# Sixty-six empty drains at the head of VectorE's program in a rotary embedding on one core

## Chip, cores, metric

One core of one Trainium2 chip. The metric is the device time of one execution in microseconds (us), the median over runs. A comparison of two kernels is a ratio with a 95% interval; it is the mean time of the one kernel's fast runs over that of the other's of the same rounds, so not quite the ratio of the medians quoted beside it.

## The reference

```python
# x: (8, 2048, 8, 64) float32; cos, sin: (2048, 32) float32
def reference(x, cos, sin):
    x1, x2 = x[..., :32], x[..., 32:]
    cos, sin = cos[None, :, None, :], sin[None, :, None, :]
    return np.concatenate([x1 * cos - x2 * sin, x1 * sin + x2 * cos], axis=-1)
```

34 MB are read and 34 MB written; there are four multiplications for each pair of values.

## The kernel before

Each of 8 batches is one tile of 128 partitions by 8192 values. Five such tiles are loaded ahead; each later load reuses a tile once its store has landed. The tables are loaded behind the first piece of batch 0. VectorE copies the cosines to PSUM first, because all its multiplies read them there:

```python
    def load(b):
        xt = xpool.tile([P, ROW], f32, tag="xt", name=f"xt{b}")
        for lo, n in spans([UNIT, UNIT, 2 * UNIT] if b == 0 else [ROW]):
            keep(nc.sync.dma_start(out=xt[:, lo : lo + n], in_=xv[b, :, lo : lo + n]))
            if b == 0 and lo == 0:
                keep(nc.sync.dma_start(out=cos_sb, in_=cos_src))
                keep(nc.sync.dma_start(out=sin_sb, in_=sin_src))
    # ... (cut)
    for b in range(NBUF):            # NBUF = 5
        load(b)
    # ... (cut: GpSimd makes an identity)
    keep(nc.scalar.mul(nsin, sin_sb, -1.0))
    keep(nc.scalar.copy(sin_ps, sin_sb))
    keep(nc.scalar.mul(neye, eye, -1.0))
    keep(nc.vector.tensor_copy(cos_ps, cos_sb))
```

For most pieces GpSimd makes x·sin into `t2`, VectorE makes x·cos into `t1` and adds the two in place. For a few pieces TensorE adds, and ScalarE copies the sum back. A batch is stored whole, except for the first and the last, which are stored in parts:

```python
    for b in range(B):
        done = 0
        outs = list(spans(shares(b)))
        for lo, n in spans(pieces(b)):
            rotate(b, lo, n)
            done = lo + n
            while outs and sum(outs[0]) <= done:
                store(b, *outs.pop(0))
        if b + NBUF <= last:
            load(b + NBUF)
```

`keep` holds an instruction at its place in the program's order. A scheduling layer adds the waits and gives out the semaphores.

Of the kernel before, what the change touches and what calls it, by code (L numbers as in the profile page):

```python
# [10 lines left out]
def kernel(  # L11
# [7 lines left out]
    nc = tc.nc  # L19
    keep = tc.keep_in_program_order  # L20
# [68 lines left out]
    keep(nc.scalar.mul(nsin, sin_sb, -1.0))  # L89
    keep(nc.scalar.copy(sin_ps, sin_sb))  # L90
    keep(nc.scalar.mul(neye, eye, -1.0))
    keep(nc.vector.tensor_copy(cos_ps, cos_sb))  # L92

    def rep(a, n):
# [125 lines left out]
```

## Time and profile before

| | before |
|---|---|
| median of the first three runs | 163.42 us (163.28 to 164.14) |
| span of the profiled run | 161.4 us |
| VectorE, GpSimd busy | 140.1 us (87%), 139.0 us (86%) |
| DMA | 67.65 MB, mean 419 GB/s |
| VectorE's copy of the cosines starts | 6.20 us |
| the last store is issued, has landed | 153.3 us, 160.6 us |

### The profile page before, as it was taken

What the parts mean: (1) busy time and instruction counts of PE and PEld (TensorE: products, weight loads), DVE (VectorE), ACT (ScalarE), POOL (GpSimd) and SP (SyncE); (2) the same over time, 40 slices, a digit from 0 to 9 for tenths busy, and PEclk for the clock granted to TensorE, in tenths of its full rate; (3) what the DMA queues carried; (4) which work ended last, traced back from release to release, by engine and by line L of the source; (5) the groups of instructions that cost most, each with busy time, mean ns of one, the idle gap of its engine ahead of it and who ended that gap; (6) DMA issues with size and microseconds to landing.
All of it is one profiled execution on the core that took longest, in us unless ns stands there. A gap on an engine that the chain in (4) does not pass through costs nothing.

```text
span 161.4 us, 467 instructions
## 1 busy us (share of the span) xinstructions
PE 46.4 (29%) x80; PEld 18.5 (11%) x80; DVE 140.1 (87%) x66; ACT 14.4 (9%) x24; POOL 139.0 (86%) x70
## 2 busy tenths in 40 slices
PE   0000000498008960893029912980000000000000
PEld 0000000133003420340014401430000000000000
DVE  0468899999999999999999999999899998999900
ACT  3200000013000220032001210140000000000000
POOL 1299999999999899998996999998999979999200
PEclk9999999999955696599755985799555555555555
DMA  5999999899999999999999999999999999999995
GB/s 181 418 445 464 449 430 390 373 427 499 406 390 447 430 487 390 447 438 414 447 422 430 447 416 438 447 406 447 455 392 455 447 398 455 438 406 455 410 398 231
DMA packets 3458, 67.65 MB, mean 419 GB/s; under 512 B 384, under 2 KB 384, under 8 KB 768
## 3 DMA queue, kind: packets, MB, share of 16 engines
q1 hardware_dynamic: 1728, 34.08, 49.8%
q10 hardware_dynamic: 1728, 33.56, 48.4%
q14 instruction: 2, 0.02, 0.0%
HBM read 34.08 MB, written 33.55 MB: 419 GB/s over the span
## 4 chain that ended last, share of the span: by engine, by line
DMA 46%; DVE 37%; POOL 9%; issue 2%; SPq 1%; DVEq 0%; POOLq 0%; ACTq 0%
DMA xt<-in_x_dram 24%; DVE t L128 18%; DMA out_dram<-xt 18%; DVE xt L135 17%; POOL t L121 9%; DMA sin_sb<-in_sin_dram 3%; DVE t L145 1%; SPq L69 0%; SPq L67 0%; DVEq L135 0%; POOLq L121 0%; ACTq L74 0%
## 5 line engine op out<-in xcount | busy, mean ns | idle before, releaser
L121 POOL TENSOR_TENSOR t<-xt,sin_sb 128x1024 f32<-128x1024 f32 (+1 forms) x32 | 70.4, 2200 | 10.7 <-DMA sin_sb<-in_sin_dram 5.7
L128 DVE TENSOR_TENSOR t<-xt,cos_ps 128x2048 f32<-128x2048 f32 (+1 forms) x34 | 73.4, 2166 | 0.8
L121 POOL TENSOR_TENSOR t<-xt,nsin 128x1024 f32<-128x1024 f32 (+1 forms) x32 | 70.4, 2200 | 0.0
L135 DVE TENSOR_TENSOR xt<-t,t 128x2048 f32<-128x2048 f32 (+1 forms) x29 | 62.2, 2144 | 6.2 <-POOL t L121 3.7
L140 PE MATMUL o<-t,eye 128*128 128x512 f32 x24 | 17.1, 803 | 25.2 <-DVE t L128 25.2
L156 PE MATMUL o<-t,eye 128*128 128x512 f32 x16 | 10.9, 781 | 36.8 <-DVE t L128 36.8
L141 PE MATMUL o<-t,eye 128*128 128x512 f32 x24 | 15.0, 710 | 0.0
L142 ACT COPY xt<-o 128x512 f32<-128x512 f32 x12 | 7.0, 586 | 46.5 <-PE o L141 46.5
L140 PEld LDWEIGHTS o<-t,eye 128*128 128x128 f32 x24 | 5.6, 247 | 33.5 <-issue 33.5
L161 ACT COPY xt<-o 128x512 f32<-128x512 f32 x8 | 4.7, 586 | 42.6 <-PE o L157 42.6
L156 PEld LDWEIGHTS o<-t,eye 128*128 128x128 f32 x16 | 3.6, 247 | 41.7 <-POOL t L121 30.6
L141 PEld LDWEIGHTS o<-t,eye 128*128 128x128 f32 x24 | 5.9, 248 | 8.5 <-issue 8.5
L92 DVE COPY cos_ps<-cos_sb 128x512 f32<-128x512 f32 x1 | 0.7, 695 | 6.2 <-DMA cos_sb<-in_cos_dram 6.2
L157 PE MATMUL o<-t,neye 128*128 128x512 f32 x8 | 4.9, 714 | 0.2 <-DVE t L145 0.2
L145 DVE TENSOR_TENSOR t<-xt,sin_ps 128x2048 f32<-128x2048 f32 x2 | 4.6, 2279 | 0.0
L157 PE MATMUL o<-t,eye 128*128 128x512 f32 x8 | 4.1, 592 | 0.0
L157 PEld LDWEIGHTS o<-t,neye 128*128 128x128 f32 x8 | 1.8, 239 | 3.6 <-issue 3.6
L157 PEld LDWEIGHTS o<-t,eye 128*128 128x128 f32 x8 | 1.5, 190 | 1.9 <-issue 1.9
L89 ACT ACT_TABLE_LOAD x1 | 1.3, 1283 | 0.7 <-PEq L204 0.7
L89 ACT ACTIVATE nsin<-sin_sb 128x512 f32<-128x512 f32 x1 | 0.6, 629 | 4.9 <-DMA sin_sb<-in_sin_dram 4.9
L90 ACT COPY sin_ps<-sin_sb 128x512 f32<-128x512 f32 x1 | 0.6, 580 | 0.0
L79 POOL MEMSET eye<- 128x128 f32 x1 | 0.2, 205 | 0.3 <-POOLq L204 0.3
(6 smaller groups left out, 1.0 us busy)
## 6 DMA issues: line engine op xcount, KB each, us to landing
xt<-in_x_dram SPq DMA_DIRECT2D x7, 4096.0 KB, 38.9
out_dram<-xt ACTq DMA_DIRECT2D x6, 4096.0 KB, 28.3
out_dram<-xt ACTq DMA_DIRECT2D x2, 2048.0 KB, 18.9
xt<-in_x_dram SPq DMA_DIRECT2D x2, 1024.0 KB, 6.0
xt<-in_x_dram SPq DMA_DIRECT2D x1, 2048.0 KB, 11.5
out_dram<-xt ACTq DMA_DIRECT2D x2, 1024.0 KB, 8.7
out_dram<-xt ACTq DMA_DIRECT2D x1, 1792.0 KB, 20.4
cos_sb<-in_cos_dram SPq DMA_DIRECT2D x1, 256.0 KB, 5.0
```

The lines of the kernel that those rows point to most:

```text
L89: keep(nc.scalar.mul(nsin, sin_sb, -1.0))
L92: keep(nc.vector.tensor_copy(cos_ps, cos_sb))
L121: nc.gpsimd.tensor_mul(out=t2u[:, :, u, :].rearrange("p (r h) d -> p r h d", h=H), in0=xu[:, :, 1 - u, :].rearrange("p (r h) d -> p r h d" ...
L128: nc.vector.tensor_mul(out=t1.rearrange("p (r k d) -> p r k d", r=nr, d=Dh), in0=xk, in1=rep(cos_ps[:, r0 : r0 + nr, :], 2 * H),)
L135: keep(nc.vector.tensor_add(out=xt, in0=t1, in1=t2))
L140: nc.tensor.matmul(o, eye, t1[:, cs], start=True, stop=False)
L141: nc.tensor.matmul(o, eye, t2[:, cs], start=False, stop=True)
L142: keep(nc.scalar.copy(xt[:, cs], o))
L145: nc.vector.tensor_mul(out=t2.rearrange("p (r k d) -> p r k d", r=nr, d=Dh), in0=xk, in1=rep(sin_ps[:, r0 : r0 + nr, :], 2 * H),)
L156: nc.tensor.matmul(o, eye, t1u[:, gs, u, :], start=True, stop=False)
L157: nc.tensor.matmul(o, eye if u else neye, t2u[:, gs, 1 - u, :], start=False, stop=True)
L161: nc.scalar.copy(xu[:, gs, u, :], o.rearrange("p (g d) -> p g d", d=Dh))
```

## The change

The intent is to learn whether instructions that do nothing, put where VectorE waits for a load anyway, are free. A drain (`nc.vector.drain()`) names no tile. The profile lists it under DVEq, with VectorE's semaphore instructions, and does not count it as busy time of VectorE, which is 140.1 us before.

```diff
     keep(nc.scalar.mul(neye, eye, -1.0))
+    for _ in range(66):
+        keep(nc.vector.drain())
     keep(nc.vector.tensor_copy(cos_ps, cos_sb))
```

## The prediction

> **What bounds the kernel now.** I read the page first for the shares of the engines and of the DMA, then the timeline of the first 22 us, because the change acts only at the head of VectorE's program, then VectorE's waits and GpSimd's, and last the chain of waits, for what an extra instruction of the sequencer costs.
>
> The page, with the busy shares (section 1), the DMA row by 40 slices of about 4 us, the traffic by queue, and the issues of the stores:
>
> ```profile
> PE 46.4 (29%) x80; PEld 18.5 (11%) x80; DVE 140.1 (87%) x66; ACT 14.4 (9%) x24; POOL 139.0 (86%) x70
> DMA  5999999899999999999999999999999999999995
> HBM read 34.08 MB, written 33.55 MB: 419 GB/s over the span
> q14 instruction: 2, 0.02, 0.0%
> out_dram<-xt ACTq DMA_DIRECT2D x2, 1024.0 KB, 8.7
> ```
>
> The reader is to see that the DMA is full from the second slice to the last but one. The bytes alone take 67.65 MB / 0.43 MB per us, about 157 us, of a span of 161.4 us (0.43 is the 429 to 448 GB/s that the windows from 7 to 131 us show). VectorE and GpSimd are nearly full too, at 87% and 86%. So the kernel is bound by transfers, with two engines close behind; a delay on VectorE counts only if it starves the store queue.
>
> The timeline of the head (start, duration, engine, what; in brackets the idle time before it and who ended it):
>
> ```profile
> 1.16 0.43 SPq L69 DMA_DIRECT2D cos_sb<-in_cos_dram  x1
> 6.20 0.69 DVE L92 COPY cos_ps<-cos_sb 128x512 f32<-128x512 f32 x1 [6.20 <-DMA cos_sb<-in_cos_dram]
> 6.93 1.23 DVE L128 TENSOR_TENSOR t<-xt,cos_ps 128x1024 f32<-128x1024 f32 x1
> 7.03 1.27 POOL L121 TENSOR_TENSOR t<-xt,sin_sb 128x512 f32<-128x512 f32 x1 [5.72 <-DMA sin_sb<-in_sin_dram]
> ...
> 9.54 1.22 DVE L135 TENSOR_TENSOR xt<-t,t 128x1024 f32<-128x1024 f32 x1 [1.38 <-POOL t L121]
> ...
> 16.53 2.29 DVE L135 TENSOR_TENSOR xt<-t,t 128x2048 f32<-128x2048 f32 x1 [0.84 <-POOL t L121]
> ```
>
> VectorE does nothing for 6.20 us, until the cosines have landed; then, after the copy and one multiply, it stands still for 1.38 us more, because GpSimd's half of the first piece is not done. It waits for GpSimd again, 0.84 us, before the add at 16.53. VectorE's own list of waits (who, for whom, total us, times, longest) has these among its five waits on GpSimd, and nothing else:
>
> ```profile
> DVE cos_ps L92 <- DMA cos_sb<-in_cos_dram: 6.2, 1, 6.2
> DVE xt L135 <- POOL t L121: 3.7, 5, 1.4
> ```
>
> The chain of waits, a stretch of it, for the price of one more sequencer instruction on VectorE (start, length, what):
>
> ```profile
> 21.16 0.03 issue
> 21.18 0.02 DVEq L135
> 21.21 0.04 issue
> 21.25 2.30 DVE xt L135
> 23.55 0.02 issue
> 23.58 2.31 DVE t L128
> ```
>
> Where a semaphore instruction (DVEq) stands between two multiplies or adds, 0.09 us pass from the end of the one (21.16) to the start of the next (21.25). Where none does, 0.03 us pass (23.55 to 23.58). So one more sequencer instruction costs about 0.06 to 0.07 us, of which its own record is only 0.02.
>
> [...] At the head VectorE has had no work, so each of these drains finds it idle already. The trace agrees that such a drain is short: the two that frame the program have records of 10 ns at 0.1 us and 19 ns at 161.0 us. [...]
>
> [...] 0.02 us recorded, 0.06 to 0.07 us spent. Whoever multiplies 66 by 10 ns gets 0.7 us and is wrong by a factor of about six.
>
> [...] In this trace the two instruction packets of the span make 0.02 MB together, so about 8 KB each[...]. No stall of VectorE in the trace can be put down to either.
>
> **The change part by part.** It removes nothing and moves no tensor instruction: in the built program VectorE keeps its 66 tensor instructions in the same order with the same waits. It adds 66 drains between the branch into the kernel and the copy of the cosines. None of them waits on a semaphore or updates one. No other engine's program changes but for the numbers of lines and buffers.
>
> *Cost of the drains.* The opening barrier lets VectorE go at about 0.7 us (the first instructions behind it on ScalarE, GpSimd and SyncE start at 0.73 to 0.74). I take 0.066 us per drain: 66 x 0.066 = 4.4 us, so they end near 5.1 us. A drain may be a little dearer than a semaphore instruction, or cheaper, being without a wait: with 0.05 us they end at 4.0, with 0.085 us at 6.3.
>
> *What lies beside other work.* All of it, in the central case: the copy cannot start before 6.20 us, as the cosines decide that. Slack left: 6.20 - 5.1 = 1.1 us. On the path: 0.
>
> *Further slack, if the drains are dearer.* Break-even for the copy is (6.20 - 0.70) / 66 = 83 ns per drain. The next 1.38 us delay the copy and the first multiply but not the first add, which waits for GpSimd: break-even (5.50 + 1.38) / 66 = 104 ns. The 0.84 us before the add at 16.53 absorb the next part: (5.50 + 1.38 + 0.84) / 66 = 117 ns. Beyond that the five gaps leave 3.7 - 1.4 - 0.8 = 1.5 us. Last, there is the queue of stores: a last store of 1024 KB takes 8.7 us from issue to landing, while its bytes at 419 GB/s take 2.5 us, so it stands about 6 us behind others (estimate from these two rows). A VectorE that ends a microsecond later mostly shortens that.
>
> *Sum.* 0 removed, 0 added on the path: 163.4 us before, 163.4 to 163.5 after. I put 163.5, leaving 0.1 us for what the instruction stream may disturb.
>
> **The rivals.**
>
> *The drains are far dearer than a sequencer instruction*, so that they outlast the wait for the cosines. For it: no run here has a drain beside a drain on VectorE, and both recorded ones are tied to barriers. Against: their records are 10 and 19 ns, as short as the semaphore instruction's 21. At 100 ns the copy would start at 7.3 us and the first add at its old time: time unchanged. At 150 ns the copy starts at 10.6 us, 4.4 late, of which 2.2 go in the first 17 us and 1.5 later: about 0.7 us remain, perhaps hidden by the queue of stores. For 2% (3.3 us) with 2.2 absorbed early, it needs (5.50 + 2.2 + 3.3) / 66 = 167 ns each. I find that unlikely.
>
> *Instruction fetch.* The program of VectorE grows by 66 instructions[...]. So a block boundary that VectorE met in mid-kernel, behind 2.3 us multiplies, may now be met at the head[...]. As an upper bound, had such a fetch to wait as long as the cosines took to land (5.0 us in the page's issues), the copy would start at 5.1 + 5.0 = 10.1 us, 3.9 late; 2.2 go in the first two waits and most of the rest later: at most 1.7 us, about 1%. A fetch of 1 us is not seen at all.
>
> *A gain.* Nothing that VectorE does at the head stands in another's way: no transfer waits for the copy, and GpSimd waits for the sines, not for VectorE. I see no way to be faster but chance in how loads and stores interleave.
>
> **Range and chances.** The three runs before lie between 163.28 and 164.14, a width of 0.5%; the central effect is 0. The range 162.9 to 164.7 holds that scatter and up to a microsecond of delay. Slower by over 2% needs 167 ns a drain or a fetch with a long stall: 0.03. Faster by over 2% has no mechanism: 0.01. Within 2%: 0.96.
>
> **What would show each step.** VectorE's records at the head of the changed trace: 66 drains, each of 10 to 20 ns, some 0.06 to 0.07 us from start to start, the last near 5.1 us. The copy starts at 6.2 us and its wait is still ended by the cosines; the first add starts at 9.5 and still waits for GpSimd. VectorE's busy time stays 140.1 us and its waits on GpSimd 3.7 us. An instruction packet may be one more or earlier. I am wrong if the copy starts after 8.4 us (6.20 + 2.2), with the drains' pitch above 117 ns or with a hole of microseconds among them; or if the copy starts on time and the span still grows, which would mean an effect outside VectorE's order that I have not seen.

The sum: the drains, 66 x 0.066 = 4.4 us, all lie beside the wait for the cosines, so it comes to 0 on the path and 163.4 to 163.5 us. The rival of instruction fetch is the author's estimate: a block boundary stands there for the place in the program at which the next packet of instructions is needed, and that 66 drains move one to the head was assumed; the 5.0 us of its upper bound are the page's.

## The result and the profile after

The changed kernel took 163.49 us in the median (163.19 to 163.96, 6 runs), the kernel before 163.37 (163.28 to 164.14, 6 runs). The ratio is 1.0003, interval 0.9979 to 1.0028: the same time.

The drains as a group, in the view of that source line (engine's queue, operation, count; shortest, median and longest record in ns; first and last start in us):

```profile
L93 DVEq DRAIN  x66: 10/10/153, 0.8 to 3.9; - x66
```

They are over at 3.9 us. The head of the timeline after:

```profile
6.33 0.69 DVE L94 COPY cos_ps<-cos_sb 128x512 f32<-128x512 f32 x1 [6.33 <-DMA cos_sb<-in_cos_dram]
...
9.60 1.22 DVE L137 TENSOR_TENSOR xt<-t,t 128x1024 f32<-128x1024 f32 x1 [1.31 <-POOL t L123]
...
16.59 2.29 DVE L137 TENSOR_TENSOR xt<-t,t 128x2048 f32<-128x2048 f32 x1 [0.84 <-POOL t L123]
```

The copy is still released by the cosines, which landed 0.13 us later in this run (the sines 0.07 later), not by the drains. The add at 9.60 still waits for GpSimd.

Two things did change. First, the waits on loads. The list of waits of the kernel before has these rows for GpSimd:

```profile
POOL t L121 <- DMA xt<-in_x_dram: 2.8, 3, 1.1
POOL t L121 <- DVE xt L135: 1.8, 2, 1.3
```

and after, GpSimd's and VectorE's:

```profile
POOL t L123 <- DMA xt<-in_x_dram: 6.4, 6, 2.4
DVE xt L137 <- POOL t L123: 4.9, 5, 1.5
```

GpSimd stood 3.6 us longer for loads, but the 1.8 us that it had stood for VectorE are gone, so it stood 1.8 us longer in all. VectorE stood 1.2 us longer for GpSimd. Yet the end did not move. The end of the timeline before (ACTq is the issue of a store):

```profile
152.07 1.23 DVE L135 TENSOR_TENSOR xt<-t,t 128x1024 f32<-128x1024 f32 x1
153.33 0.34 ACTq L74 DMA_DIRECT2D out_dram<-xt  x1
```

and after, the last add:

```profile
153.43 1.23 DVE L137 TENSOR_TENSOR xt<-t,t 128x1024 f32<-128x1024 f32 x1
```

VectorE is done 1.4 us later (154.66 against 153.30), but the last store lands at 160.8 instead of 160.6 us by the trace's landing records: it queued for a shorter time.

Second, the packets of instructions (the profile's queue q14, kind instruction; they are called fetches below). From the records of single instructions and packets in the trace:

```
VectorE's drains: starts at 0.761, 0.801, 0.840, ... 3.136 | 3.587 | 3.769, 3.809, 3.849, 3.888 us
                  39.6 ns from start to start, one hole of 451 ns before the 62nd drain, its record 153 ns
                  (the 62nd drain is the 65th instruction of VectorE's program:
                   a drain, a semaphore instruction and a branch come first;
                   the branch stands in the built program, without a record)
instruction packets inside the span, 8192 bytes each, 309 ns:   before 96.4 and 118.2 us
                                                               after   6.9 and 118.3 us
```

So one packet has moved from mid-kernel to the head. It starts 3.3 us after the hole, when the drains are over, so VectorE did not wait for it; what the hole is spent on, the trace does not tell. The landings of the loads go with the packet. The trace has 16 landing times for each of the 24 transfers (384 in all), as many as the page counts DMA engines; I read them as one of each engine, though the engines are not named. What waits for a transfer waits for the last of them: GpSimd goes on 0.13 us after the sixteenth landing of batch 7 both times (131.71 after 131.58, 133.09 after 132.96). Sorted by time, the first, the eighth, the fifteenth and the sixteenth of a load (us):

```
                      before                       after
second quarter of batch 0      8.9   9.1   9.3   9.4      8.9   9.1   9.4  10.1
batch 1                       24.3  24.4  24.6  24.7     24.3  24.4  24.7  26.2
batch 3                       53.1  53.2  53.4  53.6     53.2  53.3  53.6  55.4
batch 7                      130.6 130.8 131.3 131.6    130.7 130.9 131.4 133.0
```

Fifteen landings are within 0.2 us of where they were. One is behind the next, by 0.6 us at 10 us and by 1.6 us at the last load, and that is why GpSimd waits longer for loads. (That it is the same engine each time is likely, but not told.) The kernel absorbs it.

### The profile page after: what moved, and what is told of

Same layout as the page of the kernel before. It is cut to its first block, busy times and chain, and to the rows that moved or that the text cites. A ratio compares the mean times of both kernels' runs of the same rounds, so it can differ in the third digit from the quotient of the medians.

```text
span 161.7 us, 533 instructions
## 1 busy us (share of the span) xinstructions
PE 48.8 (30%) x80; PEld 19.4 (12%) x80; DVE 140.1 (87%) x66; ACT 14.4 (9%) x24; POOL 138.9 (86%) x70
## 4 chain that ended last, share of the span: by engine, by line
DMA 46%; DVE 37%; POOL 9%; issue 2%; SPq 1%; DVEq 0%; POOLq 0%; ACTq 0%
DMA xt<-in_x_dram 25%; DVE t L130 18%; DMA out_dram<-xt 18%; DVE xt L137 17%; POOL t L123 9%; DMA sin_sb<-in_sin_dram 3%; DVE t L147 1%; SPq L69 0%; SPq L67 0%; DVEq L137 0%; POOLq L123 0%; ACTq L74 0%
## 5 line engine op out<-in xcount | busy, mean ns | idle before, releaser
L142 PE MATMUL o<-t,eye 128*128 128x512 f32 x24 | 17.2, 809 | 23.4 <-DVE t L130 23.4
L158 PE MATMUL o<-t,eye 128*128 128x512 f32 x16 | 11.8, 843 | 37.4 <-DVE t L130 37.4
L143 PE MATMUL o<-t,eye 128*128 128x512 f32 x24 | 14.9, 709 | 0.0
L159 PE MATMUL o<-t,neye 128*128 128x512 f32 x8 | 6.3, 910 | 0.2 <-DVE t L147 0.2
L159 PE MATMUL o<-t,eye 128*128 128x512 f32 x8 | 4.1, 592 | 0.0
L159 PEld LDWEIGHTS o<-t,neye 128*128 128x128 f32 x8 | 2.5, 331 | 4.8 <-issue 4.8
```

The costliest lines, as they stand in the source:

```text
L142: nc.tensor.matmul(o, eye, t1[:, cs], start=True, stop=False)
L143: nc.tensor.matmul(o, eye, t2[:, cs], start=False, stop=True)
L158: nc.tensor.matmul(o, eye, t1u[:, gs, u, :], start=True, stop=False)
L159: nc.tensor.matmul(o, eye if u else neye, t2u[:, gs, 1 - u, :], start=False, stop=True)
```

## The experiments

Why does the time stay? Two theories, named A and B in the expectations. **A**: the transfers bound the kernel, and a late VectorE only shortens the queue of stores. **B**: the order of VectorE and GpSimd sets the end, as the chain of waits says when taken word for word, and only the waits at the head hide the drains. And how large is the margin? Each kernel below was timed in three rounds against the kernel before, which had medians of 163.41 to 163.45 us, and gave correct results.

### Twice as many drains

```diff
-    for _ in range(66):
+    for _ in range(132):
```

> Twice the drains (132) at the head. My theory: a drain costs 0.0396 us from start to start, as in the changed kernel's records, and there is a hole of about 0.45 us where the sequencer crosses a block of instructions, just before the 62nd drain, which is the 65th instruction of VectorE's program. So the 132 end at 0.76 + 131 x 0.0396 + 0.45 for one hole (6.4 us) or with a second one 64 instructions further (6.9 us). The copy then starts at 6.4 to 6.9 us, some tenths late at most, and the first add still waits for GpSimd and starts at about 9.6. Time unchanged, within 0.3%. Rival (the hole is of the clock time 3.1 to 3.6 us, not of the program's place): one hole only, same place; this run cannot separate the two by the first hole, but a second one 64 or 128 instructions further speaks for blocks. Rival for the time (any drain past the cosines lies on the path): about 0.2 to 0.7 us longer.

Measured: 164.11 us, ratio 1.0038 (1.0012 to 1.0064). The only hole lies again before the 62nd drain; the last drain starts at 6.49, the copy at 6.54 us, and the first add at 9.47. A small cost of some 0.6 us is clear of noise, although the first add is not late. I had expected none. The trace shows where it sits: of the last store fifteen landings come by 160.35 us, as in the kernel before, and the sixteenth at 161.69 instead of 160.59 us. The packets of instructions came at 6.8 and 90.2 us, and at the last load one engine was 2.6 us behind the next.

### In the middle

```diff
         for lo, n in spans(pieces(b)):
+            if b == 1 and lo == UNIT:
+                for _ in range(66):
+                    keep(nc.vector.drain())
             rotate(b, lo, n)
```

> The 66 drains in the middle, ahead of the second piece of batch 1, where VectorE has no waits. They are instructions 25 to 90 of its program. Cost: 65 x 0.0396 + about 0.1 us, and the hole: 2.7 to 3.2 us that VectorE stands still near 33 us, where it is busy otherwise. Theory of blocks: the hole lies again before the 65th instruction of the program, so before the 41st of these drains. Rival (a hole after 61 drains in a row, whatever came before): before the 62nd. Rival (a hole at 3.1 us of the clock): none. Time: theory A (transfers bound it) 163.4, within 0.4%; theory B 1 to 3 us longer.

Measured: 163.47 us, ratio 1.0004 (0.9970 to 1.0038). The timeline in the middle shows what VectorE lost, and at the end that it never made it good:

```profile
30.37 2.28 DVE L145 TENSOR_TENSOR t<-xt,sin_ps 128x2048 f32<-128x2048 f32 x1
35.87 2.30 DVE L128 TENSOR_TENSOR t<-xt,cos_ps 128x2048 f32<-128x2048 f32 x1 [3.21 <-issue]
...
154.66 1.23 DVE L135 TENSOR_TENSOR xt<-t,t 128x1024 f32<-128x1024 f32 x1
```

The first of these drains has a record of 6.64 us, which ends at 32.70 us, just after the multiply before it: it waited for VectorE to finish. Then VectorE stood still for 3.21 us in a stretch without waits and ended 2.6 us late (155.89 against 153.30). The last store was issued at 155.9 instead of 153.3 and landed at 160.63 instead of 160.59 us. Theory A holds and B falls. The hole came before the 41st of these drains, which is once more the 65th instruction of the program: a place in the program, neither a time nor a count of drains. One caution: here, as with 132 drains, the scheduling layer had given out some of the transfers' semaphores differently (see below).

### 190 and 400 at the head

```diff
-    for _ in range(66):
+    for _ in range(190):        # and, in the other kernel, 400
```

> 190 drains at the head: they end at 0.76 + 189 x 0.0396 = 8.2 us plus two or three holes of 0.45, so 9.1 to 9.6 us; the copy starts then, about 3 us late. 2.1 us of it should vanish in VectorE's two waits on GpSimd at the head (1.31 and 0.84 us in the changed kernel). Theory A (the transfers bound it and the stores queue): 163.4, unchanged within 0.3%, although VectorE runs about 1 us behind at 20 us. Theory B (VectorE's and GpSimd's order sets the end, the chain of waits being taken word for word): about 1 us longer, 0.6%.

> 400 drains at the head: they end at 0.76 + 399 x 0.0396 = 16.6 us plus 0.45 for each hole (three if one every 128 instructions, six if every 64): 17.9 to 19.3 us. The copy starts about 12 us late. Of these 2.1 go in the two waits at the head and 1.5 to 2.7 in VectorE's later waits on GpSimd, so 7 to 8 are left at the end of VectorE's work. Theory A (stores queue about 6 us behind others at the end): plus 1 to 3 us, 164.5 to 166.5. Theory B: plus 7 to 8 us, about 171. If the time rises by the full 12 us, my account of the waits that absorb is wrong.

Measured: 168.65 us with 190 (ratio 1.0315, 1.0284 to 1.0346; the profiled run took 166.59 and the other four 168.62 to 168.83), and 169.10 us with 400 (1.0339, 1.0313 to 1.0365). The 400 came out above the 1 to 3 us of theory A and below B. The 190 fit neither theory: the copy started only 3.1 us late (9.34 us), and yet they cost 5.2 us, nearly as much as 400. Holes lay before the instructions 65, 193 and 321 of the program, so one at every 128th: the theory of blocks holds for where the holes lie. It does not settle the 3%.

There was a flaw too. Comparing the built programs showed that the layer, which keeps account of the drains in its order, had given some loads and stores other semaphores, and with them other waits. With the change's 66 drains there is no such difference: apart from the drains, all five engines' programs and waits are those of before. So these runs mixed two causes, which I then took apart.

### The drains without the layer's answer, and the layer's answer without the drains

The drains are issued ahead of the scheduled program:

```diff
+    for _ in range(190):
+        nc.vector.drain()
     with _tile.TileContext(nc) as tc:
         tile_rotary_embedding_kernel(tc, *args)
```

> The 190 drains again, but issued ahead of the scheduled program, so that the scheduling layer does not see them and every engine's instructions, waits and semaphores are those of the kernel before (compared: no difference but the drains). In the run with 190 drains inside the program the layer had given the transfers' semaphores out differently, so that run mixed two causes. Drains again end near 9.2 us and the copy starts near 9.3. Theory L (the layer's other semaphores made the 3%; VectorE's late start is hidden, as in the run with the drains in the middle): 163.4, within 0.4%. Theory S (the late start, first store 1.9 us later, upsets the interleaving of loads and stores): again about 168.6, plus 3%. Theory B of before (VectorE's order sets the end): plus 1 us.

The program is scheduled with 190 drains, which are then taken out:

```diff
+    for b in nc.m.functions[0].blocks:
+        if b.name.startswith("tile_context") and not b.name.endswith("_end"):
+            kept = [i for i in b.instructions if type(i).__name__ != "InstDrain"]
+            b.instructions = kept
```

> The counterpart: the program as the layer makes it with 190 drains at the head, and the drains then taken out of it, so the transfers' semaphores and waits are those of the 190-drain run and VectorE starts at 6.3 us. Theory L: 168.6, plus 3%. Theory S: 163.4, within 0.4%. If both this and its counterpart are at 163.4, it takes the two together; then neither theory alone holds.

Measured: 168.56 us with the drains alone (ratio 1.0317, 1.0301 to 1.0333), 163.50 us with the layer's answer alone (1.0014, 0.9992 to 1.0037). Theory L falls: the semaphores are harmless, and the 3% come with the drains. The copy starts because VectorE got to it, no longer because the cosines came ("issue"):

```profile
9.33 0.69 DVE L92 COPY cos_ps<-cos_sb 128x512 f32<-128x512 f32 x1 [9.33 <-issue]
```

The end of that kernel by windows (from:to in us; busy time and count of PE, PEld, DVE, ACT and POOL; the clock; the DMA share; GB/s):

```profile
150.00:158.00 8.00, 0.00 (x0) 0.00 (x0) 7.62 (x6) 0.00 (x0) 5.51 (x5) 0.50 0.88 376
158.00:162.00 4.00, 0.00 (x0) 0.00 (x0) 0.49 (x1) 0.00 (x0) 0.00 (x0) 0.50 0.66 274
162.00:167.00 5.00, 0.00 (x0) 0.00 (x0) 0.00 (x0) 0.00 (x0) 0.00 (x0) 0.50 0.04 18
```

and of the kernel before:

```profile
150.00:158.00 8.00, 0.00 (x0) 0.00 (x0) 3.16 (x3) 0.00 (x0) 0.31 (x1) 0.50 1.00 424
158.00:162.00 4.00, 0.00 (x0) 0.00 (x0) 0.00 (x0) 0.00 (x0) 0.00 (x0) 0.50 0.40 168
```

From 162 us on only 4% of the DMA moves: about one engine of 16 still works (16 x 0.04 is 0.6). The landings say the same (first, eighth, fifteenth and sixteenth engine, us):

```
                                 before                       190 drains ahead of the program
second quarter of batch 0      8.9   9.1   9.3   9.4      8.9   9.1   9.4   9.9
second half of batch 0        13.8  14.0  14.2  14.3     13.8  14.0  14.2  15.7
batch 1                       24.3  24.4  24.6  24.7     24.0  24.2  24.5  26.1
batch 5                       91.9  92.0  92.4  92.4     89.6  89.7  91.4  95.8
batch 7                      130.6 130.8 131.3 131.6    128.3 128.5 130.9 136.8
instruction packets           96.4, 118.2                 7.3, 12.4, 120.7
```

One DMA engine falls 1.5 us behind the next by 16 us, and 5.9 us by the last load. GpSimd waits for the loads, and VectorE for GpSimd:

```profile
POOL t L121 <- DMA xt<-in_x_dram: 8.3, 6, 2.3
DVE xt L135 <- POOL t L121: 5.5, 3, 2.0
```

The last store is issued 5.2 us late (158.5 against 153.3). Its fifteenth landing comes 3.8 us later (162.4), its sixteenth only at 165.9. The fetches of VectorE's instructions, one in the changed kernel's head and two here, came under suspicion: theory F. (That they are VectorE's is inferred: in the head of these runs packets and holes number the same, one each with 66 and with 132 drains, two each with 190.) Its rival is theory S: the late start itself upsets the order of loads and stores.

### 400 drains ahead of the program

```diff
+    for _ in range(400):
+        nc.vector.drain()
```

> 400 drains ahead of the scheduled program, all waits as in the kernel before. The copy starts near 18.2 us, 12 us late, of which 2.1 vanish in the two waits on GpSimd at the head and 1.5 to 3 in the later ones; VectorE ends 7 to 9 us later, 160.5 to 162, the last store lands at least 3.9 us after that (as in the 400-drain run before, 162.56 to 166.42), plus the closing barrier: 167 to 169 us, plus 2 to 3.5%, by every theory that has the tail exposed. Theory that the late start costs its full length: 175.

Measured: 169.09 us, ratio 1.0346 (1.0331 to 1.0362), as with 400 inside the program. VectorE ends at 162.50 us, 9.2 late, and the last store lands 3.9 us after its issue. Here the end is simply VectorE's: for the last store the landings of the 16 engines lie within 0.14 us. Yet one engine had fallen behind here too, step by step: 0.6, 1.6 and 2.7 us behind the next at the loads that landed at 10.0, 15.9 and 26.7 us, after packets of instructions at 7.1, 12.6 and 19.1 us, and 4.9 us at 67.2 us. For the loads the lag was gone at 89.9 us (0.02), for the stores by the last one, so such a lag need not last to the end.

### Late drains: how much does the queue of stores hide?

```diff
+            if b == last and lo == ROW - 2 * HD:
+                for _ in range(170):
+                    keep(nc.vector.drain())
             rotate(b, lo, n)
```

> 170 drains just ahead of the last piece of the last batch, at about 150.7 us: 170 x 0.0396 plus two holes of 0.45 at most, so 6.7 to 7.6 us that VectorE stands still. The scheduled program is the same otherwise (compared). The last store, issued at 153.3 us in the kernel before and landed at 160.6, is issued at 160.0 to 160.9; it then stands behind nothing, and takes about 3.9 us (as the last one of the 400-drain run). It lands at 164 to 165: plus 3.3 to 4.3 us, 2 to 2.7%. So of about 7 us, some 3.5 are hidden in the queue of stores. If nothing were hidden: plus 7 us, 4.3%. If the queue hid 6 us as my prediction estimated: plus 1 us.

Measured: 167.16 us, ratio 1.0231 (1.0215 to 1.0246), +3.7 us, as expected. The layer's program is unchanged here apart from the drains.

```profile
157.99 1.23 DVE L128 TENSOR_TENSOR t<-xt,cos_ps 128x1024 f32<-128x1024 f32 x1 [7.29 <-issue]
159.32 1.22 DVE L135 TENSOR_TENSOR xt<-t,t 128x1024 f32<-128x1024 f32 x1
```

VectorE's end moved by 7.2 us and the kernel's by 3.7, so the queue hides 3.5 us. The last store, issued at 160.6, landed at 164.4: alone it takes 3.8 us from issue to landing, not the 2.5 us of its bytes.

### Late start without drains, drains without a late start, and both

VectorE is kept busy instead, on the tile that the copy then overwrites:

```diff
+    keep(nc.vector.memset(cos_ps, 0.0))
+    for _ in range(11):
+        keep(nc.vector.tensor_scalar_mul(cos_ps, cos_ps, 0.5))
     keep(nc.vector.tensor_copy(cos_ps, cos_sb))
```

> VectorE is kept from the copy by work instead of drains: one fill and 11 multiplies by a number on the tile of the cosines, which the copy then overwrites; no drain. 12 more instructions instead of 190, so the fetches of VectorE's instructions stay late (near 90 us), while the copy starts about as late as with 190 drains (near 9.3 us, between 6.5 and 9.5 as I do not know the length of these operations on this tile). Theory S (the late start makes the 3%): about 168.5. Theory F (the two fetches of VectorE's instructions at 6.8 and 12.5 us, while only loads run, put one of the 16 DMA engines behind, and the lag is carried to the end): 163.4 to 163.9, and the landings of the last loads lie within 1 us of each other over the 16 engines, as in the kernel before, instead of 6 to 8 us apart.

The drains go to TensorE, which has nothing to do before 30 us:

```diff
+    for _ in range(190):
+        nc.tensor.drain()
     with _tile.TileContext(nc) as tc:
```

> The 190 drains ahead of the program of TensorE instead of VectorE; TensorE's first matmul is at 30.6 us, so nothing on TensorE is late, VectorE's copy starts at 6.2 to 6.3 us, and the scheduled program is the same. TensorE's instruction blocks are fetched while the head's loads run. Theory F: one DMA engine falls behind as with 190 drains on VectorE (the landings of a load over the 16 engines 1.5 us or more apart by 16 us), and the time is 165 to 168.6. Theory S: 163.4, within 0.4%. If the lag of one engine shows but the time stays, it takes the late start and the fetches together.

Both edits together:

> Both at once, by other means than drains on VectorE: VectorE kept busy ahead of the copy, and 190 drains on TensorE. Theory S: about 168.5, as the busy one alone. Theory F: as the TensorE one alone. If the two act only together: about 168.5 here and 163.4 to 164.5 in each alone.

Measured: 163.71 us for the late start (ratio 1.0014, 0.9999 to 1.0029), 163.95 us for the drains on TensorE (1.0027, 1.0012 to 1.0042), 164.23 us for both (1.0050, 1.0031 to 1.0069). The timeline of the first of them:

```profile
0.92 0.48 DVE L92 MEMSET cos_ps<- 128x512 f32 x1 [0.92 <-PEq L207]
1.44 8.03 DVE L94 TENSOR_SCALAR cos_ps<-cos_ps 128x512 f32<-128x512 f32 x11
9.51 0.69 DVE L95 COPY cos_ps<-cos_sb 128x512 f32<-128x512 f32 x1
```

The copy starts even later than with 190 drains (9.51 against 9.33), and the kernel is within 0.3% of before: theory S falls. A start 3.3 us late is hidden, but mostly not by the queue of stores: VectorE ends at 153.88 against 153.30, so its own waits had taken up 2.7 us. Of lateness that reaches VectorE's end, the run in the middle hid 2.6 us. The fetches came at 74.9 and 116.1 us, and at the last load the slowest engine was 0.4 us behind the next.

The run with TensorE did not do what it was for. The packet that I take for TensorE's extra instructions came not at the head but at 52.9 us (one of 16384 bytes, 929 ns), so it does not test an early fetch. What it shows: 190 drains on another engine (68 ns apart for the most part) leave the slowest of the 16 engines within 0.12 us of the next up to the load that lands at 39 us; and across that fetch the slowest engine's distance to the next goes from 0.07 us (a load, landed at 53.6) to 1.2 us (a store, landed at 55.0).

### One early fetch and the late start together

```diff
+    for _ in range(66):
+        nc.vector.drain()
     with _tile.TileContext(nc) as tc:
...
+    keep(nc.vector.memset(cos_ps, 0.0))
+    for _ in range(7):
+        keep(nc.vector.tensor_scalar_mul(cos_ps, cos_ps, 0.5))
     keep(nc.vector.tensor_copy(cos_ps, cos_sb))
```

> The 66 drains of the change (one fetch of VectorE's instructions near 6.9 us, as in the changed kernel, alone worth 0) together with the late copy (a fill and 7 multiplies behind the drains; drains end near 3.9 us, the copy starts near 9.5 us, as in the run that was only kept busy, alone worth 0.1%). Theory X (the early fetch and the late start act only together): 166 to 169, plus 2 to 3%. Theory F2 (it takes two fetches at the head, as with 190 drains, and the late start adds nothing): 163.5 to 164.2, within 0.5%, and at the last load one DMA engine lies some 2 us behind, as in the changed kernel, not 6 to 8.

Measured: 164.09 us, ratio 1.0031 (1.0010 to 1.0051). The fetch came at 7.2 us, the copy started at 9.74, and at the last load the slowest engine was 0.8 us behind the next. Theory X falls: one early fetch and the late start do not make the 3% together. The lag came out smaller than the 2 us expected and than the 1.6 us of the change, so an early fetch alone does not set its size.

**What is settled and what stays open.** Settled: in the run with 190 drains one DMA engine falls behind, by 5.9 us at the last load and 3.5 us at the last store, and VectorE, which waits for those loads, issues the last store 5.2 us late. (With 190 inside the program, in the profiled run that was 2 us faster than its others, the lag at the last load was 3.8 us.) Neither the late start alone nor the changed semaphores make the 3%. The lags go with packets of instructions in most runs: 0.6 to 0.8 us behind the next after one at 6.9 us (the change), 1.5 us after the ones at 7.3 and 12.4 us, 1.2 us after the one at 52.9 with the drains on TensorE. In other runs the distance goes from 0.03 to 0.7 us across a packet at 38.3 us (in the middle), from 1.8 to 2.7 us across one at 90.2 us (132 drains), and in the kernel before from 0.01 to 0.4 us across the one at 96.4 us. But it does not grow each time: across the packet at 118.2 us in the kernel before it goes from 0.4 to 0.25 us, and after the one at 7.2 us in the last run it is 0.3 us. Open: no run had two early fetches without a late VectorE, so theory F is supported, not shown. Why the lag then grows from 1.5 to 5.9 us between 16 and 137 us, with no packet of instructions in the span between 12.4 and 120.7, I cannot say; the records do not name the engine of a packet. All these runs carried the profiler, so whether the writing of records takes part is not told either.

## Why the prediction was right

**The bound.** Right. The transfers bound the kernel, and the two runs that made VectorE late without the 190 drains (in the middle, and busy at the head) stayed within 0.2%. Delaying the last piece showed how far that goes: of 7.2 us, 3.5 were hidden.

**The cost of a drain.** Its size was off. The prediction took 0.066 us from the gap that a semaphore instruction makes between two tensor instructions. A drain that waits for nothing took 0.0396 us, with one hole of 0.45 us: over at 3.9 us, not 5.1. The error was on the safe side. The warning not to multiply the 10 ns record by 66 was right: the records sum to 0.8 us (65 x 0.010 + 0.153) and the drains took 3.1, about 4.5 times the 0.7 us, not six. The prediction also overlooked a drain: besides the two short ones, VectorE's trace before has one of 1236 ns at 152.1 us, which lasts until the last add is done at 153.3. The short records are those of drains that found VectorE idle, as at the head.

**What lies beside other work.** Right. The copy is released by the cosines, the first add by GpSimd, and VectorE's busy time is 140.1 us as before. One sign it gave did not come: VectorE's waits on GpSimd were to stay at 3.7 us, and were 4.9; the next paragraph has the reason.

**The rival of instruction fetch.** It was named as a block boundary that moves from mid-kernel to the head, and this is what happened: the packet went from 96.4 to 6.9 us. An estimate from the runs: packets of 8192 bytes (the change) and holes 128 instructions apart (the runs with 190 and 400 drains) make 64 bytes an instruction, if a packet holds what lies between two holes; the 66 drains are then half a packet. But the effect was put in the wrong place. The prediction looked for a stall of VectorE's sequencer; the hole among the drains was 0.45 us and hidden. The other effect, which goes with the packet but is not shown to come from it, was on the data: one DMA engine fell behind, by 0.6 us at 10 us and 1.6 us at the last load, and GpSimd waited 3.6 us longer for loads (1.8 us longer in all). At this size it cost nothing that the runs can tell from 0.

**The margins.** Two terms fall. The queue of stores hides 3.5 us, not 6, for two reasons of like size: the last store took 7.3 us from issue to landing (8.7 is the middle of two stores, 10.0 and 7.3), and alone it takes 3.8 us instead of the 2.5 us of its bytes. And the limit of 167 ns a drain, as a margin for any delay of the copy, held for lateness only as far as tried (3.3 us). It misses the cost that goes with the number of instructions: 190 drains, which make the copy only 3.1 us late, cost 3.1%.

## What to carry to other kernels

Price an empty instruction by the distance from start to start (39.6 ns here, of which 10 are in its record), look whether the engine waits there anyway (6.20 us here), and then look once more at what a longer program does elsewhere: here a packet of instructions moved from 96.4 to 6.9 us, and one of the 16 landings of a load came 0.6 us behind the others by 10 us, 1.6 us at the last load (that the packet holds up the data is supported here, not shown). When the transfers bound a kernel, ask how far the last store queues behind others; that is the margin of the engine in front of it (3.5 us here), and delaying the last piece alone measures it. Before an edit is read as one change, compare the built programs: a scheduling layer may answer extra instructions with other semaphores.
